# A convolution block in split fp32: the residual stored first and added to by the last transfers, and seven half-size products in one more down stage

## The chip, the cores and the metric

The kernel runs on one core of a Trainium2 chip. The metric is device time in microseconds of one execution; lower is better. Three runs of the kernel before gave a median of 1074.68 (1073.78 to 1074.71). TensorE (PE) multiplies, VectorE (DVE), ScalarE (ACT) and GpSimd (POOL) do elementwise work, and SyncE (SP) issues nearly all transfers, in one queue.

## The reference

One layer with a convolution mixer and an MLP, 256 tokens of width 2048, all in fp32:

```
cond = silu(c)
sh1, sc1, g1, sh2, sc2, g2 = split(cond @ mod_w + mod_b, 6)
h = rms_norm(x, norm1_g) * (1 + sc1) + sh1
x = x + (1 + g1) * conv_mixer(h)                       # two products, a 31-tap convolution, a layer norm
h = rms_norm(x, norm2_g) * (1 + sc2) + sh2
u = square(relu(h @ mlp_w1))                           # 2048 -> 8192
x = x + (1 + g2) * (u @ mlp_w2)                        # 8192 -> 2048
```

Only the MLP's last three quarters and the last line are touched here. The x on the right of the last line is the residual of this document; 1 + g2 is the gate, called `cb` when it is spread over 128 partitions.

## The kernel before

Every fp32 product is made of three products of split operands: an operand is hi (rounded to a type that TensorE reads at full speed) plus lo (the rest), and hi·hi, hi·lo and lo·hi are summed in PSUM (L306 to L308). Weights come from memory as tiles `raw` of 128x2048 (1 MB, seven buffers). ACT makes hi of each half tile (L232), DVE lo (L236, 128x1024), into six buffers of each kind.

The MLP goes through the 8192 inner columns in four quarters q = 0 to 3. Each quarter has an up stage (h times a quarter of mlp_w1) and a down stage (u times a quarter of mlp_w2, added into `y` in SBUF). A job is one step in these stages, with its own weights. A down job, ("down", q, i), has two weight tiles and 48 matmuls of 128x512: i // 2 is one of four blocks of 512 output columns, i % 2 the half of the inner dimension. For q < 3 the order is 0, 2, 1, 3, 4 to 7. In the up stages of q = 1, 2, 3 a part is computed with seven products of half-size blocks in place of eight (Strassen's scheme in Winograd's form, jobs "seven", named S1 to S7; U2, U3, U6, U7 are whole jobs among them). In the down stage of q = 3 four weight tiles, named x, w, z and y, are treated in the same way: seven jobs "eight" (called E here), with 12 matmuls each, stand between whole and half jobs by a list (LAST_JOBS). Their weights are sums of tiles, made by DVE in place in `raw` (a chain, L352), and some have sums of blocks of `u2` on the other side (`make_last_sums`).

The result of an up stage has tokens in partitions and must be turned. DVE transposes blocks of 32x32 (L456), SP writes the block to memory (`flat`, L457) and reads it back as eight transfers of 64 KB in pieces of 128 bytes (`two<-flat`, L474). ACT then does relu and square (L483, L484), and hi (L247), DVE lo (L250), which gives `u2`, the input of the down stage. There are four such blocks per quarter, two `u2` tiles each; in the down stage jobs 0 and 2 need blocks 0 and 1, job 1 the rest.

The residual is written to a scratch in memory, `turned`, during q = 0, in an order with features in partitions. In the down stage of q = 2 it is read back, 32 transfers of 64 KB in pieces of 128 bytes (L496), and DVE does y = y * cb and y = y + residual (`scale_y`, L1105 and L1106), 16 operations of 128x512. The down stage of q = 3 finishes each block: product times cb (L410), plus y (L411), store from SP (L412); where a block has one of the seven products, one more operation goes ahead (L409). The gates become a row `gates` in memory after down job 5 of q = 1, and are loaded as `cb` over all partitions (L1427) after job 7.

The order of instructions on each engine is fixed when the program is built. It is the order of the code's calls, with constraints (`issue_after`) and tasks put off to a later job (`at_job`). All the transfers named here are issued by SP, in the order in which they stand in its program, and an issue that must wait holds what stands behind it.

## Time and profile before

The profiled execution took 1076.49 us; its span from the first to the last instruction is 1074.5, at a mean granted TensorE clock of 0.997. The stages of the MLP that matter, from the trace (us):

| stage | from | to | length | TensorE busy | DVE busy | DMA share |
|---|---|---|---|---|---|---|
| up, q=1 | 561.7 | 643.5 | 81.8 | 81.80 | 71.97 | 0.73 |
| down, q=1 | 643.6 | 732.5 | 88.9 | 87.75 | 70.36 | 0.95 |
| up, q=2 | 732.6 | 814.5 | 81.9 | 81.81 | 74.13 | 0.84 |
| down, q=2 | 814.6 | 901.5 | 86.9 | 86.90 | 57.03 | 0.86 |
| up, q=3 | 901.6 | 984.4 | 82.8 | 82.17 | 75.98 | 0.77 |
| down, q=3, and the end | 984.5 | 1074.5 | 90.0 | 84.87 | 73.82 | 0.48 |

How to read the profile: an engine's row gives the start and length of an instruction, its line, the operation, and what it writes and reads (`lo<-raw,hi`). Behind a group stand the total and the mean in ns. A releaser in brackets, `[3.67 <-DMA two<-flat]`, is idle time ahead of the instruction and what ended it. A transfer has two times: SP's issue, and its landing. DMA share is the mean busy share of the 16 DMA engines.

### The profile page before, as it was taken

How to read it: one execution, taken by the hardware profiler on the slowest of the kernel's cores; microseconds unless marked ns; L12 is line 12 of the kernel's file. 1: busy time of each engine (PE TensorE's matmuls, PEld its weight loads, DVE VectorE, ACT ScalarE, POOL GpSimd, SP SyncE). 2: the span in 40 equal slices, each digit the busy share in tenths (PEclk: the TensorE clock that was granted, in tenths of full speed). 3: DMA queues.
4: the chain of work that ended last, by engine and by line, in shares of the span. 5: the costliest groups of instructions: out<-in, count | busy, mean ns of one | idle time of the engine just before them, and what ended most of it. 6: DMA issues, size and time to landing. Idle time of an engine off the chain costs nothing.

```text
span 1074.5 us, 15563 instructions
## 1 busy us (share of the span) xinstructions
PE 1054.7 (98%) x5868; PEld 871.6 (81%) x5868; DVE 870.6 (81%) x1135; ACT 591.3 (55%) x817; POOL 218.2 (20%) x147
## 2 busy tenths in 40 slices
PE   6999999999999999999999999999999999999998
PEld 3888886778799998888888888788888888787886
DVE  5777789988767889868788895899896678899995
ACT  4111298875875686444546574535575534556751
POOL 0000079989599262000000000000000000000000
PEclk8999999999999999999999999999999999999999
DMA  9999997996999977899895889996889983979731
GB/s 381 420 420 420 415 419 307 363 386 239 412 403 399 371 270 275 262 336 304 279 345 196 297 263 295 345 414 195 343 240 346 236 292 120 303 258 344 213 135 59
DMA packets 154333, 331.00 MB, mean 308 GB/s; under 512 B 88465, under 2 KB 114321, under 8 KB 119313
## 3 DMA queue, kind: packets, MB, share of 16 engines
q1 hardware_dynamic: 154112, 329.88, 84.9%
q8 instruction: 46, 0.75, 0.3%
q14 instruction: 29, 0.24, 0.1%
q10 hardware_dynamic: 146, 0.13, 0.0%
HBM read 313.71 MB, written 16.26 MB: 307 GB/s over the span
## 4 chain that ended last, share of the span: by engine, by line
PE 81%; DMA 9%; DVE 6%; ACT 1%; issue 1%; SPq 0%; ACTq 0%; DVEq 0%
PE mm L307 14%; PE mm L306 14%; PE mm L308 14%; DMA raw<-mod_c 7%; PE mm L264 6%; PE mm L265 3%; PE acc L261 3%; PE acc L260 3%; PE acc L262 3%; PE mm L1029 2%; PE row L516 2%; DVE lo L236 2%; PE acc L427 2%; PE acc L428 2%; PE acc L426 1%; DVE raw L608 1%
## 5 line engine op out<-in xcount | busy, mean ns | idle before, releaser
L232 ACT ACTIVATE hi<-raw 128x1024 fp32r<-128x1024 f32 x362 | 372.8, 1056 | 247.0 <-PE mm L308 159.9
L236 DVE TENSOR_TENSOR lo<-raw,hi 128x1024 fp32r<-128x1024 f32 x301 | 357.3, 1218 | 76.5 <-ACT hi L232 76.3
L306 PE MATMUL mm<-hi,u 128*128 128x512 f32 x448 | 174.2, 390 | 1.7 <-ACT hi L232 1.1
L307 PE MATMUL mm<-lo,u 128*128 128x512 f32 x448 | 174.0, 389 | 0.0
L308 PE MATMUL mm<-hi,u 128*128 128x512 f32 x448 | 173.8, 389 | 0.0
L236 POOL TENSOR_TENSOR lo<-raw,hi 128x1024 fp32r<-128x1024 f32 x61 | 157.0, 2599 | 30.7 <-ACT hi L232 30.7
L608 DVE SCALAR_TENSOR_TENSOR raw<-raw,cond 128x2048 f32<-128x2048 f32 x50 | 117.4, 2356 | 31.7 <-DMA raw<-mod_c 31.7
L308 PE MATMUL mm<-hi,hl 128*128 128x512 f32 x288 | 112.1, 389 | 0.0
L307 PE MATMUL mm<-lo,hl 128*128 128x512 f32 x288 | 112.0, 389 | 0.0
L306 PE MATMUL mm<-hi,hl 128*128 128x512 f32 x288 | 112.0, 389 | 0.0
L306 PEld LDWEIGHTS mm<-hi,u 128*128 128x128 f32 x448 | 84.1, 188 | 20.4 <-ACT hi L232 1.8
L308 PEld LDWEIGHTS mm<-hi,u 128*128 128x128 f32 x448 | 84.1, 188 | 17.9 <-DVE u L250 0.4
L307 PEld LDWEIGHTS mm<-lo,u 128*128 128x128 f32 x448 | 84.1, 188 | 17.4
L908 DVE SCALAR_TENSOR_TENSOR acc<-u,v,acc 128x256 f32<-128x256 f32 x230 | 91.6, 485 | 0.0
L264 PE MATMUL mm<-hl,hi 128*128 128x512 f32 x224 | 80.0, 401 | 0.0
L812 PE MATMUL mm<-two,first 128*128 128x256 f32 x240 | 56.7, 391 | 9.0 <-ACT two L870 9.0
L260 PE MATMUL acc<-hl,hi 128*128 128x256 f32 x224 | 63.4, 283 | 0.0
L261 PE MATMUL acc<-hl,hi 128*128 128x256 f32 x224 | 63.4, 283 | 0.0
L262 PE MATMUL acc<-hl,lo 128*128 128x256 f32 x224 | 63.4, 283 | 0.0
L306 PEld LDWEIGHTS mm<-hi,hl 128*128 128x128 f32 x288 | 54.1, 188 | 11.3
L307 PEld LDWEIGHTS mm<-lo,hl 128*128 128x128 f32 x288 | 54.1, 188 | 11.2
L308 PEld LDWEIGHTS mm<-hi,hl 128*128 128x128 f32 x288 | 54.1, 188 | 11.2
(315 smaller groups left out, 1762.0 us busy)
## 6 DMA issues: line engine op xcount, KB each, us to landing
raw<-w SPq DMA_DIRECT2D x128, 1024.0 KB, 7.3
raw<-mod_c SPq DMA_DIRECT2D x64, 1024.0 KB, 11.5
raw<-mod_r SPq DMA_DIRECT2D x28, 1024.0 KB, 9.1
raw<-w_in SPq DMA_DIRECT2D x16, 1024.0 KB, 10.8
raw<-w_out SPq DMA_DIRECT2D x16, 1024.0 KB, 8.2
first<-w_first SPq DMA_DIRECT2D x15, 1024.0 KB, 19.8
u<-kept SPq DMA_DIRECT2D x24, 512.0 KB, 7.8
flat<-two SPq DMA_DIRECT2D x30, 256.0 KB, 6.0
```

Of the source, the lines that this page charges most:

```text
L232: state["w_hi"] = nc.scalar.activation(hi, w[:, ks, :], AF.Copy).ins
L236: end = by.tensor_tensor(lo, w[:, ks, :], hi.bitcast(F32), op=ALU.subtract)
L260: nc.tensor.matmul(out_p, w, m[:, 0:T], start=begin, stop=False)
L261: nc.tensor.matmul(out_p, w, m[:, T : 2 * T], start=False, stop=False)
L262: state["mm_end"] = nc.tensor.matmul(out_p, lo[:, k % HALF, :], m[:, 0:T], start=False, stop=end)
L264: nc.tensor.matmul(p[:, c, :], hi[:, k % HALF, :], m, start=(k == 0), stop=(k == KT - 1))
L306: nc.tensor.matmul(p, p_hi, hi, start=begin, stop=False, skip_group_check=shared)
L307: nc.tensor.matmul(p, p_hi, lo, start=False, stop=False, skip_group_check=shared)
L308: nc.tensor.matmul(p, p_lo, hi, start=False, stop=end, skip_group_check=shared)
L608: end = nc.vector.scalar_tensor_tensor(w, w, 1.0, cb, op0=ALU.mult, op1=ALU.mult, accum_out=acc)
L812: step = nc.tensor.matmul(held[n][:, c, :], w[:, 2 * n + c, :], h, start=k == 0 and c == 0, stop=k == KT - 1, skip_group_check=True)
L908: end = nc.vector.scalar_tensor_tensor(out, s, w, acc, op0=ALU.mult, op1=ALU.add)
```

## The change

It has three parts, in the same program.

1. The down stage of q = 2 uses the seven products as well, on the same four tiles and with the same list of jobs: 372 matmuls in place of 384. The sums of `u2` for it are kept in space that is free at that point: `cond` (the place of `cb`), `v`, `cz`, `shz`, `rowsb`, `q5` and `two`. The load of `cb` therefore moves from the end of the down stage of q = 1 to the end of that of q = 2. A function `drain` adds the products into y.
2. The residual is no longer read back. Eight transfers (`residual_out`) copy it from the scratch to the output, memory to memory, 256 KB each in 2048 pieces of 128 bytes. They are issued by SP at the jobs in COPY_OUT, all in the up stage of q = 1. The output lies in memory in its final order (tokens by columns).
3. For the first three blocks of columns, the last stage computes (product + y) * cb on DVE, and a transfer from POOL's queue adds it to the output in memory (`accum_op`). For the last block, y * cb is made ahead, at job 3 of the last down stage, two transfers from POOL add the residual from the output to it, and the end is as it was: product times cb, plus y, store.

```diff
--- before
+++ after
...
 PLUS = {5: "w", 7: "z", 6: "z", 4: "y"}
 LAST_JOBS = (4, (1,), 6, (5,), (7,), (3,), 5, (6,), (2,), 1, (4,), 3, 7)
+EIGHT = (2, 3)
 TILE_OF = {"x": (2, 0), "w": (0, 0), "z": (0, 1), "y": (2, 1)}
 MORE = {(0, 0): (1, ALU.add), (0, 1): (5, ALU.add), (1, 1): (7, ALU.subtract)}
+ADDED = 3
+COPY_OUT = [("up", 1, m) for m in (2, 3, 6, 7)] + [("seven", 1, m) for m in (3, 6, 2, 4)]
 OPERAND = {1: "x", 5: "x", 6: "x", 4: "x", 7: "w", 3: "z", 2: "y"}
...
 
     def regions(job):
-        if job[:2] != ("down", QUARTERS - 1):
+        if job[0] == "up" or job[1] not in EIGHT or job[1] < QUARTERS - 1 and job[2] >= 4:
             p = ps.tile([P, 2, 2 * T], F32, name="mm", bufs=2)
...
             at = HALF * (job[2] % 2) + k
             m = acts_of[at // 2][:, at % 2, :]
-            begin, end = at == 0 or job == ("down", QUARTERS - 1, 1) and t == 1 and at == HALF, at == KT - 1
-            shared = job[:2] == ("down", QUARTERS - 1)
+            shared = job[0] == "down" and job[1] in EIGHT
+            begin, end = at == 0 or shared and job[2] == 1 and t == 1 and at == HALF, at == KT - 1
             p_hi, p_lo = [m[:, n : n + P] for n in (t * P, T + t * P)]
...
         if m == 1:
             run_tasks()
-        split_w(("eight", m), nc.vector, chain[name])
+        split_w(("eight", q, m), nc.vector, chain[name])
         if m in (7, 4):
...
 
-    def mm_eight(p, m):
+    def mm_eight(p, q, m):
         for k in range(4):
-            hi, lo = [w[:, 4 * (k % 2) : 4 * (k % 2) + 4, :].rearrange("p k n -> p (k n)") for w in parts["eight", m][k // 2]]
+            hi, lo = [w[:, 4 * (k % 2) : 4 * (k % 2) + 4, :].rearrange("p k n -> p (k n)") for w in parts["eight", q, m][k // 2]]
             if m in (1, 2, 4):
                 at, t = k + (0 if m == 1 else 4), P if m == 4 else 0
                 p_hi, p_lo = [u2[at // 2][:, at % 2, n : n + P] for n in (t, T + t)]
             else:
-                t = P if m in (7, 3) else 0
-                p_hi, p_lo = [last_sums[k // 2, m in (6, 3)][:, k % 2, n : n + P] for n in (t, T + t)]
+                p_hi, p_lo = [s[:, k % 2, :] for s in half_sums[k // 2, m]]
             begin, end = k == 0 and m not in (2, 3), k == 3
...
         return parts_of
 
-    def make_last_sums(k2):
-        work = [acts.tile([P, 2, 2 * T], F32, name="hl", bufs=HALF) for _ in range(2)]
-        _, _, c, d = four_sums(u2[k2], u2[2 + k2], [w[:, :, n : n + T] for w in work for n in (0, T)])
-        for j, src in enumerate((c, d)):
-            last_sums[k2, bool(j)] = acts.tile([P, 2, 2 * T], F32R, name="hl", bufs=HALF)
-            split_act(last_sums[k2, bool(j)], src)
+    def pairs_in(s, n):
+        return [s[:, 2 * T * j : 2 * T * j + 2 * T].rearrange("p (a t) -> p a t", a=2) for j in range(n)]
+
+    def homes(q, k2):
+        if q == QUARTERS - 1:
+            both = [acts.tile([P, 2, 2 * T], F32R, name="hl", bufs=HALF) for _ in range(2)]
+            return [(s[:, :, 0:T], s[:, :, T : 2 * T]) for s in both]
+        if k2 == 0:
+            s = pairs_in(const.tile([P, KT, P], F32R, name="cond").rearrange("p k n -> p (k n)"), 4)
+        else:
+            s = pairs_in(const.tile([P, NVEC], F32R, name="v"), 2)
+            s += pairs_in(const.tile([P, KT, 35], F32R, name="cz").rearrange("p k n -> p (k n)"), 1)
+            s += pairs_in(x_pool.tile([P, KT, 32], F32R, name="shz").rearrange("p k n -> p (k n)"), 1)
+        return [s[0::2], s[1::2]]
+
+    def make_half_sums(q, k2):
+        if q == QUARTERS - 1:
+            work = acts.tile([P, 2, 2 * T], F32, name="hl", bufs=HALF)
+            a, b = work[:, :, 0:T], work[:, :, T : 2 * T]
+        elif k2 == 1:
+            a, b = two(), two()
+        else:
+            work = tmp.tile([P, 512], F32, name="rowsb", bufs=1), mp.tile([P, 512], F32, name="q5", bufs=1)
+            a, b = [s.rearrange("p (a t) -> p a t", a=2) for s in work]
+        for dst, src in ((a, u2[k2]), (b, u2[2 + k2])):
+            nc.vector.tensor_tensor(dst, src[:, :, 0:T].bitcast(F32), src[:, :, T : 2 * T].bitcast(F32), op=ALU.add)
+        (a0, a1), (b0, b1) = [(s[:, :, 0:P], s[:, :, P : 2 * P]) for s in (a, b)]
+        for dst, y0, y1 in ((b1, a1, b1), (a1, a1, a0), (a0, a0, b1), (b0, b0, a0)):
+            nc.vector.tensor_tensor(dst, y0, y1, op=ALU.subtract)
+        for src, (hi, lo), ms in zip((b, a), homes(q, k2), ((3, 5), (6, 7))):
+            nc.scalar.activation(hi, src, AF.Copy)
+            state["sums_end"] = nc.vector.tensor_tensor(lo, src, hi.bitcast(F32), op=ALU.subtract).ins
+            for h, m in enumerate(ms):
+                half_sums[k2, m] = [s[:, :, h * P : h * P + P] for s in (hi, lo)]
 
...
         nc.vector.tensor_tensor(kept_of[5], kept_of[5], w, op=ALU.add)
+
+    def drain(n, t, cs, p):
+        s = y[:, t, 512 * n + cs.start : 512 * n + cs.stop]
+        with tc.issue_after(state["y_end"].ins) if "y_end" in state else ExitStack():
+            state["y_end"] = nc.vector.tensor_tensor(s, p, s, op=ALU.add)
+            if (n, t) in MORE:
+                m, op = MORE[n, t]
+                state["y_end"] = nc.vector.tensor_tensor(s, s, kept_of[m], op=op)
 
...
                 m, op = MORE[n, t]
                 nc.vector.tensor_tensor(g, p, kept_of[m], op=op)
-            nc.vector.tensor_tensor(g, g if (n, t) in MORE else p, cb[:, at], op=ALU.mult)
+                p = g
+            if n < ADDED:
+                nc.vector.tensor_tensor(g, p, s, op=ALU.add)
+                p = g
+            state["y_end"] = nc.vector.tensor_tensor(g, p, cb[:, at], op=ALU.mult)
+        if n < ADDED:
+            nc.gpsimd.dma_start(rows_out[:, t, at], g, accum_op=ALU.add)
+            return
         state["y_end"] = nc.vector.tensor_tensor(s, s, g, op=ALU.add)
-        nc.sync.dma_start(out[:, t, at], s)
+        nc.sync.dma_start(rows_out[:, t, at], s)
+
+    def residual_out(b):
+        with tc.issue_after(state["load"].ins):
+            nc.sync.dma_start(
+                out[32 * b : 32 * b + 32, :].rearrange("p (f t) -> p f t", t=32),
+                turned[:, :, 32 * b : 32 * b + 32].rearrange("k (a p) t -> p (k a) t", p=32),
+            )
 
...
             k2 = 2 * n + h
             u2[k2] = mp.tile([P, 2, 2 * T], F32R, name="u2", bufs=HALF)
-            split_act(u2[k2], s)
-
-    def fetch(n):
-        pieces = []
-        for t in range(2):
-            b = two().rearrange("p a t -> p (a t)")
-            for g in range(4):
-                nc.sync.dma_start(
-                    b[32 * g : 32 * g + 32, :].rearrange("p (a t) -> p a t", t=32),
-                    turned[4 * n : 4 * n + 4, :, 32 * (4 * t + g) : 32 * (4 * t + g) + 32].rearrange("k (a p) t -> p (k a) t", p=32),
-                )
-            pieces.append(b)
-        return pieces
+            with tc.issue_after(state["sums_end"]) if (q, n) == (2, 2) else ExitStack():
+                split_act(u2[k2], s)
 
...
         else:
             jobs += [("up", q, i) for i in range(HALF)]
-        if q < QUARTERS - 1:
+        if q in EIGHT:
+            jobs += [("eight", q) + m if isinstance(m, tuple) else ("down", q, m) for m in LAST_JOBS]
+        else:
             jobs += [("down", q, i) for i in (0, 2, 1, 3, 4, 5, 6, 7)]
-        else:
-            jobs += [("eight",) + m if isinstance(m, tuple) else ("down", q, m) for m in LAST_JOBS]
     def by_tokens(job):
...
             turn_out(flat, t, p)
         if n == 3:
-            read_block(at + (4 if q == QUARTERS - 1 else 1), q, n, flat)
+            read_block(at + {2: 5, 3: 4}.get(q, 1), q, n, flat)
         else:
...
             nc.vector.tensor_tensor(kept_of[7], bank[4], kept_of[7], op=ALU.subtract)
             turn_out(kept_of["flats"][0], 1, kept_of[7])
-            read_block(at + (3 if q == QUARTERS - 1 else 2), q, 2, kept_of["flats"][0])
-
-    def scale_y(s, at, piece):
-        nc.vector.tensor_tensor(s, s, cb[:, at], op=ALU.mult)
-        nc.vector.tensor_tensor(s, s, piece, op=ALU.add)
-
+            read_block(at + (3 if q in EIGHT else 2), q, 2, kept_of["flats"][0])
+
+    rows_out = out.rearrange("(t p) d -> p t d", t=2)
     tasks = {}
     state["job"] = KT + HALF - 2
-    chain, sums_of, kept_of, last_sums = {}, {}, {}, {}
+    chain, sums_of, kept_of, half_sums = {}, {}, {}, {}
 
...
                 copy_wide(COPY_AT[n], False)
         kind, i = job[0], job[-1]
+        if job in COPY_OUT:
+            residual_out(COPY_OUT.index(job))
         if kind == "seven":
...
             elif i % 2 and job[1] in SEVEN:
                 at_job(n + 1, block_out, n + 1, job[1], i // 2, sums.pop((kind, i // 2)))
-                for k2 in range(2) if job == ("up", QUARTERS - 1, 7) else ():
-                    at_job(n + 1, make_last_sums, k2)
+                for k2 in range(2) if i == 7 and job[1] in EIGHT else ():
+                    at_job(n + 1, make_half_sums, job[1], k2)
             elif i % 2:
...
                 with tc.issue_after(state["load"].ins):
                     nc.sync.dma_start(gates[0].rearrange("(k p) -> p k", p=P), modc[:, G2 * KT : G2 * KT + KT])
-            if job == ("down", 1, 7):
+            if job == ("down", 2, 7):
+                cb = const.tile([P, KT, P], F32, name="cond").rearrange("p k n -> p (k n)")
                 with tc.issue_after(state["load"].ins):
                     nc.sync.dma_start(cb, gates.to_broadcast([P, D]))
-            if job[1] == 2 and i % 2 == 0:
-                with tc.issue_after(state["load"].ins):
-                    pieces[i // 2] = fetch(i // 2)
+            if job == ("down", QUARTERS - 1, 3):
+                for t in range(2):
+                    last_y = y[:, t, 512 * ADDED :]
+                    with tc.issue_after(state["w_lo"]):
+                        nc.vector.tensor_tensor(last_y, last_y, cb[:, 512 * ADDED :], op=ALU.mult)
+                    nc.gpsimd.dma_start(last_y, rows_out[:, t, 512 * ADDED :], accum_op=ALU.add)
             if i % 2 == 0:
...
                 if job[1] == 0:
                     nc.scalar.activation(s, p, AF.Copy)
-                elif job[1] < QUARTERS - 1:
+                elif job[1] not in EIGHT:
                     state["drain"] = nc.vector.tensor_tensor(s, p, s, op=ALU.add).ins
-                    if job[1] == 2 and i < HALF - 1:
-                        scale_y(s, at, pieces[i // 2][t])
-                    elif job[1] == 2:
-                        at_job(n + 4, scale_y, s, at, pieces[i // 2][t])
-                elif i in (1, 5):
-                    at_job(n + 1, finish, i // 2, t, cs, p)
                 else:
-                    finish(i // 2, t, cs, p)
+                    end = finish if job[1] == QUARTERS - 1 else drain
+                    if i in (1, 5):
+                        at_job(n + 1, end, i // 2, t, cs, p)
+                    else:
+                        end(i // 2, t, cs, p)
 
```

The order of SP's program around the end of the up stage of q = 1 and the first jobs of the down stage. Names: `raw<-w` is a weight tile, `raw<-mod_c` a weight tile of the gates, `flat<-two` a block written to be turned, `two<-flat` its reading, `out<-turned` a piece of the residual. Before:

```order
L208 DMA raw<-w 128x2048 x3
L457 DMA flat<-two 128x4x128
L208 DMA raw<-w 128x2048 x2
L457 DMA flat<-two 128x4x128
L208 DMA raw<-mod_c 128x2048 x2
L474 DMA two<-flat 32x16x32 x8
```

Now:

```order
L461 DMA out<-turned 2048x1x32
L211 DMA raw<-w 128x2048
L461 DMA out<-turned 2048x1x32
L211 DMA raw<-w 128x2048 x2
L461 DMA out<-turned 2048x1x32
L509 DMA flat<-two 128x4x128
L211 DMA raw<-w 128x2048 x2
L461 DMA out<-turned 2048x1x32
L509 DMA flat<-two 128x4x128
L211 DMA raw<-mod_c 128x2048 x2
L461 DMA out<-turned 2048x1x32
L526 DMA two<-flat 32x16x32 x8
```

Five of the eight pieces now stand among these rows, all ahead of the eight readings; the other three stand earlier in the stage.

DVE's program near the middle of the down stage of q = 2. `x` is y's place, `lo<-raw,hi` a split of half a weight tile, `raw<-raw` a sum of weight tiles. Before:

```order
L236 TENSOR_TENSOR lo<-raw,hi 128x1024 x10
L1105 TENSOR_TENSOR x_2504<-x_2504,cond 128x512 x2
L236 TENSOR_TENSOR lo<-raw,hi 128x1024 x2
L1106 TENSOR_TENSOR x_2504<-x_2504,two 128x512 x2
L236 TENSOR_TENSOR lo<-raw,hi 128x1024 x3
```

Now:

```order
L239 TENSOR_TENSOR lo<-raw,hi 128x1024
L355 TENSOR_TENSOR raw<-raw 128x2048
L429 TENSOR_TENSOR pad<-acc,rowsb 128x512
L430 TENSOR_TENSOR q_7425<-q_7425,pad 128x512
L239 TENSOR_TENSOR lo<-raw,hi 128x1024 x5
L435 TENSOR_TENSOR x_2504<-row,x_2504 128x512
L438 TENSOR_TENSOR x_2504<-x_2504,rowsb 128x512
L435 TENSOR_TENSOR x_2504<-acc,x_2504 128x512
L239 TENSOR_TENSOR lo<-raw,hi 128x1024
L438 TENSOR_TENSOR x_2504<-x_2504,q_7425 128x512
```

The scaling by the gates and the addition of the residual are gone from here; in their place stand sums of weight tiles, what follows the eighth products, and additions into y with a second term.

22 lines of the change are left out of this document (10 added, 12 removed).

## The prediction

> **What bounds the kernel now.** I read first the busy times on the page, then the MLP by its six stages (up and down of quarters 1, 2 and 3, a view by stretches), then TensorE's waits in the MLP, and last the queue around the places where the change adds work.
>
> ```profile
> PE 1054.7 (98%) x5868; PEld 871.6 (81%) x5868; DVE 870.6 (81%) x1135; ACT 591.3 (55%) x817; POOL 218.2 (20%) x147
> ```
>
> TensorE (PE) is busy for 98% of the span of 1074.5. The stages, with the columns stretch, length, busy time (instructions) of PE, weight loads, DVE, ACT and POOL, granted clock, DMA share and GB/s:
>
> ```profile
> 561.70:643.50 81.80, 81.80 (x361) 67.43 (x360) 71.97 (x65) 52.70 (x60) 0.00 (x0) 1.00 0.73 248
> 643.60:732.50 88.90, 87.75 (x385) 71.75 (x384) 70.36 (x75) 40.15 (x44) 0.00 (x0) 1.00 0.95 338
> 732.60:814.50 81.90, 81.81 (x361) 67.42 (x360) 74.13 (x69) 52.07 (x58) 0.00 (x0) 1.00 0.84 281
> 814.60:901.50 86.90, 86.90 (x385) 71.97 (x384) 57.03 (x58) 40.29 (x44) 0.00 (x0) 1.00 0.86 266
> 901.60:984.40 82.80, 82.17 (x361) 67.39 (x361) 75.98 (x72) 51.84 (x58) 0.00 (x0) 1.00 0.77 254
> 984.50:1074.50 90.00, 84.87 (x373) 69.53 (x371) 73.82 (x83) 43.36 (x51) 0.00 (x0) 1.00 0.48 157
> ```
>
> Two readings. Row four, the down stage of q=2, has no idle TensorE at all: 384 matmuls in 86.90, that is 0.2263 us each, so each matmul left out there is worth 0.2263 us if nothing else comes late. Row two, the down stage of q=1, is the one in which the DMA engines have nothing to spare: share 0.95. What stalls TensorE in the MLP is small; columns: total, times, longest.
>
> ```profile
> PE mm L306 <- ACT hi L232: 1.1, 1, 1.1
> PE mm L306 <- DVE two L456: 0.6, 1, 0.6
> PE row L426 <- DMA u<-kept: 0.5, 1, 0.5
> ```
>
> So the number of matmuls sets the time as long as splits, transposes and transfers keep a small lead. The question is which lead the change uses up.
>
> **Matmuls removed: -2.7.** The eight half-tile products that four of q=2's down tiles need (96 matmuls) become seven eight-jobs of 12 each (84). 12 x 0.2263 = 2.7 us.
>
> **Vector work added in q=2's down stage: nothing but one stall of 0.6.** Prices by form, from the groups of DVE from 600 us on (busy, mean ns):
>
> ```profile
> L236 DVE TENSOR_TENSOR lo<-raw,hi 128x1024 fp32r<-128x1024 f32 x209 | 247.9, 1218 | 65.0 <-ACT hi L232 65.0
> L352 DVE TENSOR_TENSOR raw<-raw 128x2048 f32<-128x2048 f32 x4 | 9.1, 2286 | 0.0
> L1106 DVE TENSOR_TENSOR x<-x,two 128x512 f32<-128x512 f32 x8 | 5.3, 684 | 0.0
> L386 DVE TENSOR_TENSOR hl<-hl 128x256 f32<-128x256 f32 x8 | 3.2, 416 | 0.0
> L250 DVE TENSOR_TENSOR hl<-hl 128x512 fp32r<-128x512 f32 x4 | 2.8, 689 | 0.0
> L380 DVE TENSOR_TENSOR hl<-u 128x512 f32<-128x512 f32 x4 | 2.6, 687 | 0.0
> ```
>
> Added: three more weight tiles to split (seven operands out of four tiles), 6 halves x 1.22 = 7.3; four chain sums x 2.29 = 9.1; the half sums of u2 for two k2, each 2 x 0.69 + 4 x 0.42 + 2 x 0.69 = 4.4, so 8.8; three operations after job E6 and three extra drains, 6 x 0.68 = 4.1. Removed: the 16 operations of scale_y (L1106's eight and as many multiplications of the same form), 10.9. Net +18.4: 57.0 becomes 75.4 in a stage of 84.2, 90%. The row of up in q=2 shows 74.1 in 81.9 without a stall, so this can be carried; q=3's down, which runs the same job list, shows one stall for a late transpose, the 0.6 us of the waits above. I take that 0.6 here too. Below nothing it cannot go (the stage has no stall to lose); above, I let it be 2.0, because here the half sums' places (cond, v, cz, shz) are in other buffers and four lo halves of a job stand behind them. ACT gets six more hi, 6 x 1.06, at 40 of 87 us busy: nothing.
>
> **The fetches that go: -0.5.** Before, 32 transfers of 512 pieces bring the residual in, the last eight of them among the first weights of up q=3; columns start, us:
>
> ```profile
> 914.50 2.30 SPq L496 DMA_DIRECT2D two<-turned  x4
> 916.90 2.00 SPq L208 DMA_DIRECT2D raw<-w  x1
> 918.94 2.71 SPq L496 DMA_DIRECT2D two<-turned  x4
> ...
> 923.82 0.85 SPq L444 DMA_DIRECT2D u<-kept  x2
> ```
>
> The sums that they push back (u<-kept) are what TensorE waited for, 0.5 us, in that stage. I take it as gone. The gates' broadcast of 1 MB now stands a quarter later, in the start of up q=3; in the same place of up q=2 it hid (81.81 of 81.90 busy). The one wait added there is for `cond`, which now holds half sums until the eight-jobs have run; the last of them stands two whole down jobs before that load, so the weights queued behind it on SP aren't held. Nothing for it.
>
> **The residual stored ahead: +7.7.** This is the large term. Eight transfers from DRAM to DRAM (out<-turned, 2048 pieces of 128 bytes each) go into SP's queue in up q=1; by the order, five of them stand between the last weights and transposes of that stage, which in the trace are these, and all ahead of the eight two<-flat at 652.41:
>
> ```profile
> 632.10 1.58 SPq L208 DMA_DIRECT2D raw<-w  x3
> 633.78 0.46 SPq L457 DMA_DIRECT2D flat<-two  x1
> 635.26 2.60 SPq L208 DMA_DIRECT2D raw<-w  x2
> 641.89 0.38 SPq L457 DMA_DIRECT2D flat<-two  x1
> 644.13 3.20 SPq L208 DMA_DIRECT2D raw<-mod_c  x2
> 652.41 7.16 SPq L474 DMA_DIRECT2D two<-flat  x8
> ```
>
> In this very stretch the engines have no room (first row: a stretch with room, where the third of the eight falls; the first two stand still earlier; I put all three at nothing, and they cost their length each, some 6 us in all, if the weights then had no lead):
>
> ```profile
> 605.00:610.00 5.00, 5.00 (x23) 4.14 (x23) 3.50 (x5) 3.40 (x4) 0.00 (x0) 1.00 0.46 129
> 630.00:635.00 5.00, 5.00 (x24) 4.14 (x23) 5.00 (x6) 4.51 (x6) 0.00 (x0) 1.00 0.94 238
> 640.00:645.00 5.00, 5.00 (x24) 4.14 (x23) 4.45 (x6) 4.00 (x5) 0.00 (x0) 1.00 1.03 397
> ```
>
> The flat written at 641.89 landed 10.5 us after its issue, at 652.4, and SP issued the reads of it at 652.41, at once:
>
> ```profile
> L457 SPq DMA_DIRECT2D flat<-two x1: 377/377/377, 641.9 to 641.9; - x1
> ...
> DMA to landing us min/median/max: 6.0/8.3/10.5
> ```
>
> So whatever is put ahead of it in this queue moves it by its full length, if the queue is served in order. What is late next: the block's read, its relu and square, its hi and lo, and then TensorE, in whose down job 1 this block is the first input.
>
> ```profile
> 662.83 0.68 DVE L250 TENSOR_TENSOR u<-two,u 128x512 fp32r<-128x512 f32 x1
> 643.60 0.39 PE L306 MATMUL mm<-hi,u 128*128 128x512 f32 x1
> ```
>
> The lo is ready at 663.51; jobs 0 and 2 cover until 643.60 + 96 x 0.2263 = 665.3. The lead is 1.8 us.
>
> One residual transfer, p: the nearest rows are the pieces of 128 bytes of two<-flat. From 618.5 to 621.8 nothing else ran:
>
> ```profile
> q1 hardware_dynamic: 2276, 0.28, 56.6%
> ```
>
> 2276 packets in 56.6% of 16 engines x 3.3 us is 13.1 ns each; 128 pieces per engine make 1.68 us, the lower bound. Issuing such pieces took 2.30 us for four transfers of 512 (the row at 914.50), and 7.16 for eight in the row at 652.41, 3.58 per 2048. I take 1.9: the queue is backed up there, so engines decide and not the issue, with a little for pieces that are written to DRAM as well. 5 x 1.9 - 1.8 = +7.7. After that the weights behind are as late as TensorE is, so they add nothing more.
>
> Against this change speaks the Trainium skill, "DMA: Bandwidth & Descriptors", Specifications: a transfer needs at least 512 bytes for line rate, and below that the DMA does a read-modify-write. By it a 128-byte piece written to DRAM would cost more than one read from it; the trace has such small writes only in the gates (below), which were slow, so it agrees as far as it goes. By that rule the sum would be rival C's.
>
> **The end: nothing.** Three of four blocks of columns now leave through accumulating transfers from POOL, six of 256 KB. The last column ends as before (multiplication, the addition at 1070.72, its store); the last accumulate comes from the column before, and two more bring the residual into the last column of y, behind the last lo:
>
> ```profile
> 1054.77 1.23 DVE L236 TENSOR_TENSOR lo<-raw,hi 128x1024 fp32r<-128x1024 f32 x1 [0.46 <-ACT hi L232]
> ...
> 1061.22 0.69 DVE L411 TENSOR_TENSOR x<-x,two 128x512 f32<-128x512 f32 x1
> ...
> 1065.28 0.69 DVE L411 TENSOR_TENSOR x<-x,two 128x512 f32<-128x512 f32 x1
> ...
> 1070.72 0.69 DVE L411 TENSOR_TENSOR x<-x,two 128x512 f32<-128x512 f32 x1
> ...
> out<-x SPq DMA_DIRECT2D x8, 256.0 KB, 2.0
> ...
> gates<-modc SPq DMA_DIRECT2D x1, 8.0 KB, 17.5
> ```
>
> The last accumulate has from 1061.9 to the span's end at 1074.5 as cover, 12.6 us, for what takes 2.0 as a plain store. Those into y stand behind two more multiplications (0.7 each) after the lo of 1054.77, so from 1057.4 to the addition at 1065.28: 7.9 us. If they took as long as the slowest small transfer, 17.5, the end would come 9.6 late, and if they gain nothing it is 0; they are whole rows of 2 KB as the store's are, so I take 0. "DMA: Bandwidth & Descriptors" of the Trainium skill, Anatomy of one DMA — SWDGE (gpsimd) path, would give an estimate of 2.6 us for 256 KB, which no run here shows for an accumulate.
>
> **Sum.** -2.7 + 0.6 - 0.5 + 7.7 = +5.1. The profiled execution took 1076.49 with its span of 1074.5; 2.0 lie around the span. It would become a span of 1079.6 and 1081.6. The profiled one stands 1.8 above the median of the three runs, 1074.68, so the time forecast is 1079.8. Its own range: four transfers of 1.68 give 6.7 - 1.8 = +4.9 in place of 7.7, 1077.0; five of 3.58 give 17.9 - 1.8 = +16.1, 1088.2.
>
> **Rivals.**
> B, the delay is hidden, and the change is faster. It decides where the five together push the flat back by less than 1.8 us, so below 0.4 each: if the backlog at 641.89 is only weights fetched ahead, and transfers share the engines rather than queue. For it: share 0.46 at 605, so part may land earlier; TensorE was never idle in this stage. Against: the landing after 10.5 us. Then -2.7 + 0.6 - 0.5 = -2.6: 1072.1. Chance 0.27.
> D, DVE bounds the new down stage. For it: 90% busy over the whole, and the half sums and chain sums crowd in its first two thirds. Against: up q=2. With the delay hidden and stalls of 3.2 in place of 0.6 it comes to 1074.7. Chance 0.12.
> C, pieces of 128 bytes are slow to write. For it: the gates' 2048 pieces of 4 bytes took 17.5 us to land while the queue carried little else. From 727 to 738:
>
> ```profile
> q1 hardware_dynamic: 2221, 0.84, 65.1%
> ```
>
> 65.1% of 16 x 11 us over 2221 packets is 52 ns each, 6.6 us for 128 per engine. 5 x 6.6 - 1.8 = 31, so 1074.7 - 2.6 + 31 = 1103. Against: 4 bytes are far from 128, and two<-flat moves 128 at 13.1 ns. Chance 0.07.
> E, the end waits for accumulates, the delay being hidden: with half of the 9.6, -2.6 + 4.8 = +2.2, 1076.9. For it: POOL issues no transfer in this part of the trace, and none accumulates. Against: the cover. Chance 0.08.
> The forecast itself (A): 0.46.
>
> **Range and chances.** 0.2% (2.1 us) is about what a measurement of this kernel can tell from no change. Faster needs B with its stall small: 0.21. Same: the rest of B (0.06), most of D (0.10), half of E (0.04) and a little of the forecast (0.02): 0.22. Slower: the rest of the forecast, C and what is left of D and E: 0.57. The range takes in B below (1072.1, and 1.1 for the stall of 0.6 and the 0.5 not being there) and the forecast's upper bound of 1088 with some of C: 1071 to 1091.
>
> **What would show it.** After the change the last flat of up q=1 lands about 20 us after its issue and TensorE stalls 6 to 9 us near 665, ended by ACT or DVE for that u2: A. A stall there under 1 us: B. DMA share near 1 with few GB/s from 631 on and a stall over 20: C. The down stage of q=2 should be 84.2 to 86 long with 372 matmuls; longer by DVE's waits: D. Between the last finish and the end of the span 3 us as before; more: E. If the five transfers land spread out and the flat still lands within 12 us, my reading of the queue is wrong.

## The result, and the profile after

The changed kernel takes 1088.37 us (median of 4, 1086.27 to 1088.90) beside 1074.26 (4 runs of the kernel before, 1073.78 to 1074.71): a ratio of 1.0128, 95% interval 1.011 to 1.0145, so 14.1 us slower where 5.1 were forecast. Its profiled execution is the shortest of the four, 1086.27 with a span of 1084.5; that of the kernel before was, at 1076.49, longer than its timed runs. The two traces therefore explain 10.0 us (spans 1074.5 and 1084.5); the other 4 lie between executions of the same kernel and are taken up at the end of the experiments.

The page of the changed kernel, first section, and its six stages from q=1 on (same columns as before):

```profile
PE 1055.8 (97%) x5856; PEld 870.6 (80%) x5856; DVE 890.8 (82%) x1153; ACT 598.5 (55%) x829; POOL 223.9 (21%) x155
```

```profile
561.30:643.18 81.88, 81.88 (x361) 67.51 (x360) 72.72 (x65) 51.83 (x59) 0.00 (x0) 1.00 0.83 252
643.18:740.86 97.68, 89.54 (x385) 73.28 (x384) 70.50 (x76) 41.12 (x46) 0.00 (x0) 0.97 0.96 335
740.86:822.84 81.98, 81.90 (x362) 67.51 (x360) 74.38 (x69) 52.05 (x58) 0.00 (x0) 1.00 0.81 270
822.84:910.20 87.36, 85.96 (x373) 69.55 (x372) 76.33 (x79) 48.75 (x56) 0.00 (x0) 1.00 0.72 246
910.20:992.22 82.02, 81.94 (x362) 67.42 (x360) 74.09 (x69) 51.93 (x58) 0.00 (x0) 1.00 0.76 265
992.22:1084.50 92.28, 84.89 (x373) 69.55 (x371) 74.55 (x84) 42.85 (x51) 7.22 (x8) 0.97 0.57 158
```

Set beside the rows of before, three stages differ. Down q=1 grew from 88.9 to 97.7. Down q=2 should have shrunk from 86.9 to 84.2 and is 87.4: 12 matmuls fewer, and all of their 2.7 us lost again, with some 0.4 more. The last stage grew from 90.0 to 92.3. Up q=3 is 0.8 or 0.9 shorter. The longest waits of TensorE are

```profile
PE mm L309 <- ACT u L250: 7.3, 1, 7.3
PE mm L310 <- DVE lo L239: 1.1, 1, 1.1
PE mm L309 <- DVE x L1482: 0.8, 1, 0.8
```

The first and the third stand in down q=1, the second in down q=2.

**Down q=1.** SP's queue around the last flats of up q=1 (start, length of the issue):

```profile
642.78 0.55 SPq L461 DMA_DIRECT2D out<-turned  x1
643.42 6.24 SPq L509 DMA_DIRECT2D flat<-two  x1
649.75 1.28 SPq L211 DMA_DIRECT2D raw<-w  x2
651.08 0.55 SPq L461 DMA_DIRECT2D out<-turned  x1
651.73 5.96 SPq L509 DMA_DIRECT2D flat<-two  x1
657.78 0.95 SPq L211 DMA_DIRECT2D raw<-mod_c  x2
658.79 0.55 SPq L461 DMA_DIRECT2D out<-turned  x1
660.04 9.39 SPq L526 DMA_DIRECT2D two<-flat  x8
```

The issue of a copy takes 0.55, but the transfer behind it isn't taken for 6 us: the two flats hold SP for 6.24 and 5.96 where they took 0.46 and 0.38. I read this as a queue that has no room left; no view shows its filling. The second flat lands 8.3 us after the start of its issue (651.73 + 8.3 = 660.0), before it landed at 652.4: 7.6 us later, behind four copies (the fifth stands behind this flat and ahead of its reading). So one copy costs 1.9 us. TensorE stands still for 7.3 us, and then something follows that the waits don't show. Stretches of the stall, of what comes behind it, and of the eight-jobs in down q=2:

```profile
664.70:672.40 7.70, 0.41 (x2) 0.00 (x0) 0.01 (x1) 2.45 (x5) 0.00 (x0) 0.82 0.89 174
672.40:676.70 4.30, 4.29 (x11) 3.34 (x12) 3.79 (x5) 3.96 (x5) 0.00 (x0) 0.53 1.00 361
850.00:856.00 6.00, 4.60 (x16) 2.50 (x15) 6.00 (x8) 6.00 (x10) 0.00 (x0) 1.00 0.86 332
```

In the second row the granted clock is 0.53: from the first matmul behind the stall, at 672.41, to the one at 676.69 ten steps take 4.3 us where 2.3 were due, 2.0 us on top of the stall. The Trainium skill, "TensorE: Matmul & The Clock Gate", Part 1: The HAM clock gate, states such a rule: after an idle window of about 3.4 us the clock is halved until TensorE has been busy for about as long. By that rule a stall of 7.3 us carries a slow stretch with it; the trace agrees, 7.3 us idle and 4.3 at about half. The rule does not cover what the first experiment below shows, where two stalls of 1.2 us halve the clock as well.

**Down q=2.** The third row: from 850 to 856 DVE is busy for all of 6.00 us, ACT as well, and TensorE for 4.60. The row alone doesn't tell which of the two TensorE is behind.

**The end.** POOL's transfers, and the last addition on DVE:

```profile
1066.28 0.88 POOL L1473 DMA_DIRECT2D x<-out  x1 [3.32 <-issue]
1070.61 0.90 POOL L1473 DMA_DIRECT2D x<-out  x1 [3.45 <-issue]
1074.95 0.88 POOL L454 DMA_DIRECT2D out<-two  x1 [3.44 <-issue]
1079.16 0.89 POOL L454 DMA_DIRECT2D out<-two  x1 [3.34 <-DVE x L456]
```

```profile
1077.95 0.69 DVE L456 TENSOR_TENSOR x<-x,two 128x512 f32<-128x512 f32 x1
```

They start 4.3 us apart though their data were ready long before (the last one's at 1069.1, by the order of DVE's operations). From the end of the last addition to the end of the span it is 5.9 us (1078.6 to 1084.5); before it was 3.1 (1071.4 to 1074.5).

So the 10.0 us are: -2.7 for the matmuls, +7.5 the stall (its step less one matmul), +2.0 the slow clock, -0.8 for small stalls of down q=1 that went or moved, +3.1 lost in down q=2 (what is left of that stage; its matmuls' steps show 2.7 of it between 850 and 856), -0.9 in up q=3, -0.5 for the stall of the last stage that is shorter, +2.8 at the end, and -0.4 ahead of these stages: 10.1. (Stages are counted from first matmul to first matmul; before, these stood at 561.7, 643.6, 732.6, 814.6, 901.6 and 984.5.)

### The profile page after: what moved, and what is told of

Its sections match the earlier page's. It is cut to its first block, busy times and chain, and to the rows that moved or that the text cites. A ratio compares the mean times of both kernels' runs of the same rounds, so it can differ in the third digit from the quotient of the medians.

```text
span 1084.5 us, 15550 instructions
## 1 busy us (share of the span) xinstructions
PE 1055.8 (97%) x5856; PEld 870.6 (80%) x5856; DVE 890.8 (82%) x1153; ACT 598.5 (55%) x829; POOL 223.9 (21%) x155
## 4 chain that ended last, share of the span: by engine, by line
PE 73%; DMA 11%; DVE 9%; issue 2%; ACT 2%; SPq 2%; POOLq 0%; POOL 0%; ACTq 0%; DVEq 0%
PE mm L310 11%; PE mm L311 11%; PE mm L309 11%; DMA raw<-mod_c 7%; PE mm L267 6%; PE mm L268 3%; DVE lo L239 3%; PE acc L264 2%; PE acc L263 2%; PE acc L265 2%; PE mm L1070 2%; DMA flat<-two 2%; DVE raw L649 2%; PE row L557 2%; SPq L526 2%
## 5 line engine op out<-in xcount | busy, mean ns | idle before, releaser
L235 ACT ACTIVATE hi<-raw 128x1024 fp32r<-128x1024 f32 x368 | 377.2, 1054 | 231.8 <-PE mm L311 124.7
L239 DVE TENSOR_TENSOR lo<-raw,hi 128x1024 fp32r<-128x1024 f32 x307 | 363.4, 1216 | 49.7 <-ACT hi L235 49.0
L309 PE MATMUL mm<-hi,u 128*128 128x512 f32 x384 | 150.5, 393 | 8.4 <-ACT u L250 7.3
L310 PE MATMUL mm<-lo,u 128*128 128x512 f32 x384 | 150.2, 391 | 1.1 <-DVE lo L239 1.1
L311 PE MATMUL mm<-hi,u 128*128 128x512 f32 x384 | 149.5, 391 | 0.0
L454 POOL DMA_DIRECT2D out<-two x6 | 5.4, 906 | 653.8 <-DVE two L452 642.2
L309 PEld LDWEIGHTS mm<-hi,u 128*128 128x128 f32 x384 | 72.6, 189 | 25.2 <-ACT u L250 7.7
L310 PEld LDWEIGHTS mm<-lo,u 128*128 128x128 f32 x384 | 72.6, 189 | 16.7 <-DVE lo L239 1.6
L311 PEld LDWEIGHTS mm<-hi,u 128*128 128x128 f32 x384 | 72.5, 189 | 15.1 <-DVE u L253 0.2
L310 PEld LDWEIGHTS mm<-lo,hl 128*128 128x128 f32 x288 | 54.1, 188 | 11.3
L309 PEld LDWEIGHTS mm<-hi,hl 128*128 128x128 f32 x288 | 54.1, 188 | 11.2
```

The lines of the kernel that those rows point to most:

```text
L235: state["w_hi"] = nc.scalar.activation(hi, w[:, ks, :], AF.Copy).ins
L239: end = by.tensor_tensor(lo, w[:, ks, :], hi.bitcast(F32), op=ALU.subtract)
L309: nc.tensor.matmul(p, p_hi, hi, start=begin, stop=False, skip_group_check=shared)
L310: nc.tensor.matmul(p, p_hi, lo, start=False, stop=False, skip_group_check=shared)
L311: nc.tensor.matmul(p, p_lo, hi, start=False, stop=end, skip_group_check=shared)
```

## The experiments

The theory after this: each copy ahead of the last flat costs 1.9 us of queue, and the stall brings the slow clock; POOL's transfers run one after another; DVE is too busy in down q=2. The first rivals: the copies cost wherever they stand, and the loss in down q=2 comes from being late. Each run was timed beside the kernel before, whose median lay between 1074.26 and 1075.71, and the ratios go by that; a difference of about 1 us between the medians of two runs says little. The 2.2 and 9.7 in some expectations are the slow clock and the loss of down q=1 as they were first read; by the matmuls' steps they are 2.0 and 9.5.

**Copies moved to three up stages.**

```diff
-COPY_OUT = [("up", 1, m) for m in (2, 3, 6, 7)] + [("seven", 1, m) for m in (3, 6, 2, 4)]
+COPY_OUT = [(kind, q, m) for q in (1, 2, 3) for kind, m in (("up", 2), ("seven", 3), ("up", 3))][:8]
```

> All eight residual copies stand behind the second, third and early jobs of the up stages of quarters 1, 2 and 3 (three, three and two), none near the last flats of up q=1. Theory (each copy ahead of the last flat delays it by 1.95 us in SP's queue; five of them less a lead of 1.8 made the 7.5 us stall, and the slow clock behind it 2.2 more): the stall at 664.7 and the stretch at clock 0.53 go, 9.7 us less, about 1078.7. Rival 1 (the DMA engines' total work counts, not the place in the queue): the loss moves into up q=2 and q=3 with their shares of 0.84 and 0.77, time 1086 to 1088. Rival 2 (128-byte writes slow the memory): the same 1086 to 1088, with stalls wherever the copies stand.

Measured: 1083.76 (1080.78 to 1084.84), ratio 1.0079 (1.0066 to 1.0092). The stall of 7.3 and its slow clock are gone, but only 4.6 us of 9.5 came back. In its trace up q=1 is 0.7 longer than in the changed kernel's, up q=2 1.3 and down q=2 2.8. In down q=2 its waits are now

```profile
PE mm L310 <- DVE lo L239: 1.2, 1, 1.2
PE acc L375 <- ACT v L421: 1.2, 1, 1.2
PE mm L309 <- ACT u L250: 1.1, 1, 1.1
```

The last is the first input of that stage, late behind the copies in up q=2. The two others fall within 2 us and halve the clock for 8 matmuls (427 ns from one to the next). Part of rival 1 holds: copies cost in up q=2 too, by delaying u2.

**The transfers into y ahead of all stores.**

```diff
-            if job == ("down", QUARTERS - 1, 3):
+            if job == ("down", QUARTERS - 1, 4):
```

> The two transfers that add the residual into the last block of y are made at the first job of the last down stage in place of its job 3, so that they stand ahead of all six accumulating stores on POOL's queue. Theory (these transfers run one after another, 4.3 us apart, whatever their data; the last one is late because of the two in front of it): the last accumulate lands before the last plain store, 2.8 us less, 1085.6. Rival (an accumulating store is slow in landing by itself, or POOL's end of program takes the time): unchanged, 1088.4.

Measured: 1084.69 (1082.74 to 1086.09), ratio 1.009 (1.0076 to 1.0103); 3.7 below the changed kernel. POOL's last two, in its trace:

```profile
1068.41 0.87 POOL L454 DMA_DIRECT2D out<-two  x1 [4.51 <-DVE two L452]
1072.65 0.88 POOL L454 DMA_DIRECT2D out<-two  x1 [3.37 <-issue]
```

They are still 4.2 apart, but the last one is out before the last addition (1078.9), and the span ends 3.2 us after that, as in the kernel before. The last stage takes 89.8 where the changed kernel's took 92.3. The term for the end is shown.

**Seven products undone in q=2.**

```diff
-EIGHT = (2, 3)
+EIGHT = (3,)
...
-            read_block(at + {2: 5, 3: 4}.get(q, 1), q, n, flat)
+            read_block(at + {3: 4}.get(q, 1), q, n, flat)
```

The constraint that held back the third block's u2 goes with them.

> The seven half-size products are undone in q=2 (the residual part of the change stays). Theory (the products saved 2.7 us of TensorE and lost 2.9 to a DVE that was busy without a gap from 844 to 860): 1088.4 + 2.7 - 2.9 = 1088.2, no stall in the down stage of q=2, 86.9 long. Rival (those stalls come from the stage being late and out of step after the 7.5 us stall, not from DVE's load): a loss of 2.7 shows, 1091, or stalls in the plain stage as well.

Measured: 1087.84 (1086.34 to 1089.56), ratio 1.0121 (1.0108 to 1.0134), so no difference from the changed kernel. But the stage wasn't free of stalls, against the expectation:

```profile
PE mm L309 <- ACT u L250: 1.5, 1, 1.5
```

That is the fourth block's u2, read behind two weight tiles. The products gained nothing here, for this and for the reason expected; this run doesn't separate the two, the one with the copies moved as well, further on, does.

**The kernel before, once more** (no edit).

> The kernel before itself, for a second profile beside the first (whose execution, 1076.5, was 2.2 above the median of its runs): 1074.3 in the median; if its stalls of 1.3 at 689 and 0.9 at 930 are steady they are there again, and if they are what made the first profile longer, they are gone.

Measured: 1074.44 (12 runs, 1073.15 to 1076.92). In its trace, with a span of 1073.0, the waits are

```profile
PE mm L306 <- ACT hi L232: 1.2, 1, 1.2
PE mm L306 <- DVE two L456: 0.6, 1, 0.6
```

The wait for hi, at 689 in the first trace, is there again. The wait for `u<-kept` (0.5) isn't. It belonged to that execution, and the gain booked on it, 0.5, was mostly not to be had.

**Two copies in place of five.**

```diff
+COPY_OUT = [("up", 1, 2), ("up", 1, 3)] + [("seven", 1, m) for m in (3, 2, 4)] + [("eight", 2, m) for m in (6, 2, 4)]
```

> Of the five residual copies ahead of the last flats of up q=1 only two stay there; the three early ones of that stage stay too, and the other three go to the end of the down stage of q=2, where the readings of the residual stood in the kernel before. Theory (1.95 us each, lead 1.8): the stall before the third block's u2 falls from 7.5 to 2 x 1.95 - 1.8 = 2.1, and a stall that short leaves no stretch at half clock behind it (2.2): 1088.4 - 5.4 - 2.2 = 1080.8. Rival (the delay does not go by the number of copies; any copy in front of the flat holds the queue till it has landed, about 8 us): stall of 5 or more, 1086.

Measured: 1082.49 (1082.24 to 1085.05), ratio 1.0079 (1.0062 to 1.0095). The stall ahead of the third block is 1.9 us of waiting, 2.05 by the matmuls' steps, where 2.1 was expected:

```profile
PE mm L309 <- ACT u L250: 2.5, 2, 1.9
```

(the second wait in this row, 0.6, is the next block's). Behind it the clock stays at 1.00:

```profile
667.00:671.00 4.00, 3.98 (x16) 3.02 (x17) 3.22 (x4) 3.86 (x5) 0.00 (x0) 1.00 1.01 395
```

Five copies gave 7.5, two give 2.05: 1.8 us each, and the line crosses zero at 0.9 copies, which is a lead of 1.6 us beside the 1.8 of the prediction. The time is 1.7 above the expected one: down q=2 takes 89.3 in this trace, 1.9 more than in the changed kernel's.

**The same bytes in large pieces.**

```diff
-                out[32 * b : 32 * b + 32, :].rearrange("p (f t) -> p f t", t=32),
-                turned[:, :, 32 * b : 32 * b + 32].rearrange("k (a p) t -> p (k a) t", p=32),
+                out[32 * b : 32 * b + 32, :].rearrange("p (f t) -> (p f) t", t=256),
+                turned[2 * b : 2 * b + 2].rearrange("k p t -> (k p) t"),
```

> The eight copies stay at their places with the same 256 KB each, but move contiguous memory, 16 pieces of 16 KB, in place of 2048 of 128 bytes; so the residual lands in another order and the output is not the reference's. Theory (a copy costs by its pieces): 256 KB at the 400 GB/s that the queue reaches there is 0.66 us, twice that if reading and writing share the engines; 5 x 1.0 - 1.8 = 3.2 for the stall in place of 7.5, and less of the half clock: 1082 to 1084. Rival (a copy from memory to memory costs by its bytes or by a fixed time): stall 7.5, 1088.4.

Measured: 1078.99 (1078.22 to 1079.22), ratio 1.0037 (1.0023 to 1.005), 9.4 below the changed kernel. The wait for u2 isn't among its waits at all:

```profile
PE mm L310 <- DVE lo L239: 1.1, 1, 1.1
PE acc L376 <- DVE lo L239: 0.8, 1, 0.8
PE acc L375 <- ACT v L421: 0.7, 1, 0.7
```

I had expected 3.2. The last two flats of up q=1 hold SP for 0.53 and 0.38 us only, and the reading of the block begins at 651.81, no later than before. So with the same places and bytes the copies cost less than the lead, under 0.4 each. The cost goes with the 2048 small pieces and not with the bytes.

**All copies in down q=2, and the transfers into y ahead.**

```diff
+COPY_OUT = [("eight", 2, m) for m in (3, 6, 2, 4)] + [("down", 2, m) for m in (5, 1, 3, 7)]
```

> All eight copies in the down stage of q=2, behind the five first of its jobs (where the kernel before read the residual), and the transfers into the last block of y at the first job of the last stage. Theory: the 9.7 at 665 to 677 go, and no up stage gets a new stall (as up q=2 did when the copies were put there); the end is 3.7 shorter, as measured alone: 1088.4 - 13.4 = 1075.0, with DVE's stall of 2.9 in the down stage of q=2 left; 1078 if the clock falls there as it did with the copies in the three up stages. Rival (copies cost wherever they stand): 1079 or more, with new stalls in the down stage of q=2 or in up q=3.

Measured: 1077.12 (1076.43 to 1079.76), ratio 1.0025 (1.0014 to 1.0035). 11.3 of the 14.1 are back. What its trace, the longest of its nine executions, lost anew is in up q=3, in SP's queue and in its waits there:

```profile
915.49 5.68 SPq L461 DMA_DIRECT2D out<-turned  x2
921.22 1.36 SPq L1467 DMA_DIRECT2D cond<-gates  x1
922.67 0.85 SPq L211 DMA_DIRECT2D raw<-w  x2
```

```profile
PE mm L309 <- ACT hi L235: 1.0, 1, 1.0
PE mm L310 <- DVE lo L239: 0.8, 1, 0.8
```

Two copies and cb's load stand ahead of the weights; two stalls close together, and again the half clock behind them.

**Half of the half sums on POOL.**

```diff
+        by = nc.gpsimd if q == 2 and k2 == 1 else nc.vector
...
-            nc.vector.tensor_tensor(dst, y0, y1, op=ALU.subtract)
+            by.tensor_tensor(dst, y0, y1, op=ALU.subtract)
```

> As the kernel with the copies in the down stage of q=2 and the early transfers into y, and the second half of the half sums of q=2 (two additions, four subtractions, two lo) computed by POOL, which does nothing there, in place of DVE. Theory (the stalls at the eight-jobs M5 and D6 of q=2 are DVE's, which is busy without a gap from 844 to 860, with 4.4 us of these sums among them): the stall falls from 2.9 to under 0.8, about 1072.5. Rival (POOL's slower operations, 2.6 us where DVE takes 1.2, or a port that both share, make the sums or DVE later): the stall stays or grows, 1075 to 1078.

Measured: 1080.18 (1079.09 to 1080.59), ratio 1.0047 (1.0034 to 1.006), 3.1 worse than without. POOL started late and was slow, and DVE was slow beside it:

```profile
833.64 4.15 POOL L417 TENSOR_TENSOR two<-u 128x512 f32<-128x512 f32 x2 [421.37 <-DMA flat<-two]
837.86 6.07 POOL L420 TENSOR_TENSOR two<-two 128x256 f32<-128x256 f32 x4
843.90 1.26 POOL L423 TENSOR_TENSOR shz<-two,v 128x512 fp32r<-128x512 f32 x1
```

```profile
834.96 3.38 DVE L253 TENSOR_TENSOR u<-two,u 128x512 fp32r<-128x512 f32 x2
838.26 5.09 DVE L239 TENSOR_TENSOR lo<-raw,hi 128x1024 fp32r<-128x1024 f32 x3
```

DVE's two 128x512 took 1.69 each (0.69 elsewhere), its splits 1.70 (1.22). That is the rival. The Trainium skill, "Trainium Architecture — The Big Picture", What this means for kernel authors, says that DVE and GpSimd share a port and exclude one another there; the trace agrees in that both are slower together: POOL's two 128x512 took 2.07 us each, and one of that size at 843.90, with DVE idle, took 1.26.

**Three copies in up q=1, five in down q=2.**

```diff
+COPY_OUT = [("up", 1, 2), ("up", 1, 3), ("seven", 1, 3)] + [("eight", 2, m) for m in (3, 6, 2)] + [("down", 2, m) for m in (5, 1)]
```

> The three copies of up q=1 that cost nothing stay there, the other five go to the middle of the down stage of q=2 (none next to the loading of cb), and the early transfers into the last block of y. Theory: what the kernel with all eight in the down stage still lost in up q=3 (two stalls of 1.1 and 1.0 and 1.7 of half clock, since two copies and cb's 1 MB stood together ahead of that stage's weights) goes, 3.9 of its 1077.1: 1073.2, beside 1074.9 for the kernel before. Rival (that loss comes from cb's load alone, which the kernel before had a quarter earlier): 1077.

Measured: 1076.57 (11 runs, 1075.34 to 1079.14) beside 1075.70, ratio 1.0011 (1.0002 to 1.002). The stalls of up q=3 are gone, but its trace, the longest of its executions, has waits that the changed kernel's did not have, one at the start of down q=1 (645.6) and one in up q=1 (630.8):

```profile
PE mm L309 <- ACT u L250: 1.1, 1, 1.1
PE acc L479 <- DVE lo L239: 0.7, 1, 0.7
```

By the steps of the matmuls, six of the twelve traces with copies in up q=1 lose 0.7 to 1.9 us at the start of down q=1, and none of the four without. So the three copies that I had put down as free are so only in some executions. The larger loss is in down q=2, 89.4 long.

**The same without the seven products**, with copies in ("down", 2, 1), 3, 4, 5 and ("up", 3, 2).

> The same care for the copies (three in up q=1, four in the down stage, one in up q=3) and the early transfers into y, with the seven products of q=2 undone. Theory (they save 2.7 and lose 2.9 to DVE): the same time as with them, 1073.4, plus up to 1.6 for the third-block stall that the kernel without the products showed at 856: 1073 to 1075. Rival (the products' loss was due to the lateness in q=1): without them 2.7 slower, 1076 or more.

Measured: 1076.45 (12 runs, 1075.71 to 1080.40), ratio 1.0012 (1.0003 to 1.0022): with and without the products the time is the same, and the residual part by itself, placed with care, gains nothing over the kernel before. In the stage itself the traces differ: down q=2 takes 87.0 here, without a stall, and 89.4 with the products above. So the products cost more there than they save, and the loss of 3.1 in the changed kernel's trace was a small one: in the seven other traces with these products and this order of jobs, all sums made by DVE, the stage takes 88.3 to 90.1. As the late stall is gone from five of the seven, being late isn't the cause. What the run without the products loses elsewhere, some of it in its longer down q=1 (90.6 for 88.5), was not followed up.

**One set of half sums left out.**

```diff
+        if q < QUARTERS - 1 and k2 == 1:
+            half_sums.update({(1, m): half_sums[0, m] for m in (3, 5, 6, 7)})
+            return
```

> As the first of these, but q=2's second set of half sums is left out and the first one used in its place (eight operations of DVE, 4.4 us, and two of ACT less; the result is not the reference's). Theory (the stalls before and in the eight-jobs of q=2 are DVE's load): they fall from 2.9 to under 0.8, about 1071. Rival (they come from late weight tiles or from TensorE's waits for ACT): they stay, 1073.

Measured: 1072.87 (7 runs, 1071.94 to 1074.89) beside 1075.70, ratio 0.9974 (0.9963 to 0.9986), and no wait at all in down q=2, which takes 84.6. The middle of that stage in the kernel with three copies in up q=1 and both sets of sums, and here:

```profile
812.00:860.00 48.00, 45.15 (x191) 35.29 (x191) 42.18 (x48) 29.92 (x40) 0.00 (x0) 1.00 0.85 284
812.00:860.00 48.00, 48.00 (x212) 39.53 (x211) 42.63 (x44) 30.94 (x39) 0.00 (x0) 1.00 0.84 273
```

Eight operations of DVE, 4.4 us, and two of ACT decide over the 2.7 us of the matmuls. Which of the two engines it is stays open: of the three long waits in the first of these traces two end with DVE's splits and one with ACT, both engines lost work by this edit, and in the changed kernel both were busy without a gap from 850 to 856.

**D5 ahead of E5** (the eight-job called M5 in the expectation), with the second set of half sums behind, or between, the splits of the third and fourth block. Both blocks are also read one or two jobs earlier, the constraint on u2 is gone, and one of the five copies stands at another job.

```diff
+MID_JOBS = (4, (1,), 6, 5, (5,), (7,), (3,), (6,), (2,), 1, (4,), 3, 7)
...
-                    at_job(n + 1, make_half_sums, job[1], k2)
+                    at_job(n + (1 if job[1] == QUARTERS - 1 or k2 == 0 else 5), make_half_sums, job[1], k2)
```

> As the kernel with three copies in up q=1, five in the down stage and the early transfers into y; in the down stage of q=2 whole job D5 now stands ahead of eight-job M5, and the second set of half sums is made behind the splits of the third and fourth block. So the half sums are wanted 48 matmuls (10.9 us) later, and DVE's work is the same. Theory (in the first 25 us of that stage DVE has more to do than time before M5; with the sums out of that stretch the stall goes, as when they were left out): 2.9 less than with the old order, about 1073 to 1073.7, beside 1075 to 1075.7 for the kernel before. Rival (DVE's total in the stage, 75.4 of 84.2, is too much in any order): stalls of 2 to 3 elsewhere in that stage, 1076.

> The same, with the second set of half sums one task earlier, between the splits of the third and the fourth block. Theory: as above, within 1 us, with a small stall for the fourth block's u2, which stands behind three of these operations; 1073 to 1074.5. Rival: 1076.

Measured: 1081.12 (1080.15 to 1083.13), ratio 1.0054 (1.0041 to 1.0067), and 1078.10 (1076.70 to 1080.81), ratio 1.0032 (1.002 to 1.0044). In the down stage, the first and then the second of them:

```profile
PE acc L376 <- ACT hi L236: 3.4, 1, 3.4
PE acc L376 <- ACT v L422: 1.0, 1, 1.0
```

```profile
PE acc L378 <- DVE shz L423: 1.7, 1, 1.7
PE mm L312 <- DVE u L254: 1.4, 1, 1.4
```

The stalls move and stay: the rival. In the two orders tried, with the reads moved too, the place doesn't help; what helped was less work. Both waits of the first order end with ACT, so DVE alone isn't shown to be the cause.

**POOL's transfers without adding.**

```diff
-            nc.gpsimd.dma_start(rows_out[:, t, at], g, accum_op=ALU.add)
+            nc.gpsimd.dma_start(rows_out[:, t, at], g)
...
-                    nc.gpsimd.dma_start(last_y, rows_out[:, t, 512 * ADDED :], accum_op=ALU.add)
+                    nc.gpsimd.dma_start(last_y, rows_out[:, t, 512 * ADDED :])
```

> The changed kernel with its eight transfers on POOL's queue made plain (they store or load without adding, so the residual is lost in the output and the result is not the reference's); data, places and queue are the same. Theory: the 4.24 us from one to the next belong to POOL's queue, whatever the transfer does: the last four stand 4.2 apart again and the end is as late, 1088. Rival: adding is what makes one wait for the other, so plain ones follow each other within 1.0 (POOL's issue is 0.9), the end is 2.8 shorter, 1085.

Measured: 1088.72 (1086.05 to 1088.98), ratio 1.0116 (1.0098 to 1.0133). The time is not clearly different (1.0128 for the changed kernel), but the trace settles the question it was run for:

```profile
1069.38 1.15 POOL L1473 DMA_DIRECT2D x<-out  x2 [1.73 <-DVE x L1472]
1072.64 0.55 POOL L454 DMA_DIRECT2D out<-two  x1 [2.10 <-DVE two L452]
```

Two in a row take 1.15, the span ends 3.2 us after the last addition, and the last stage takes 90.5 for 92.3. It is the adding, not POOL's queue, that sets them 4.3 apart, and my theory on that point was wrong. In place of the 2.7 saved this trace has a longer stall at 675 (8.3), one of 1.2 at the start of down q=1, and 0.7 at 1006. All three stand ahead of POOL's first transfer, at 1045.1, so the edit didn't make them.

**The other 4 us.** Up to the last stage the programs of "the transfers into y ahead" and "without adding" are the changed kernel's, so their traces are two more executions of it. From the start of up q=1 to the start of down q=3 they take 431.4 and 435.2 us, the changed kernel's own trace 430.9. The second is 4.3 longer: 1.4 at the end of up q=1, 1.3 in down q=1 and 1.5 in down q=2. So one program does differ by this much from one execution to the next, and in the stages named above: a wait of nothing to 1.2 us at the start of down q=1, 8 to 14 slow matmuls behind the long stall, 2.7 to 4.3 us lost before and in the eight-jobs. The changed kernel's profiled execution was the shortest on each count or close to it.

**What stays open** is why one execution has these waits and another doesn't, and whether DVE or ACT is what TensorE is behind in down q=2.

## Why the prediction was wrong

The direction and the main mechanism were right, the size was not: +5.1 was forecast, +14.1 measured, +10.0 between the traces. What failed are three terms of the sum that stood at nothing or near it: what follows the stall, the vector work, and the end. The time came out at the upper end of the forecast's own range (1088.2), but not for the reason given there: no copy took 3.58.

- *Residual stored ahead, +7.7*: right. The stall measured 7.5; 1.8 to 1.9 us per copy and a lead of 1.6 to 1.8 held, with five copies and with two. The 1.9 had been chosen between 1.68 and 3.58, so that it came so close is in part luck. Of the signs named for it the stall showed and the landing did not: the flat landed 8.3 us after its issue, not 20, and the copies spread out, from 639.6 to 667.6, which by the prediction's last sentence would make its reading of the queue wrong. The order was as read, for these transfers landed in the order of their issues; but the waiting was on SP, ahead of the flat's issue, which began at 651.73 in place of 641.89. That the cost is in the pieces was shown by the large ones. Rival C (slow writes) fell: a piece copied within DRAM costs 1.9 us / 128 = 15 ns, near the 13.1 of a piece read into SBUF. Rival B fell with the landing at 660.0.
- *What follows a stall of that length*: left out of the sum. The clock fell to 0.53 for 4.3 us, 2.0 us more. The sentence "After that the weights behind are as late as TensorE is, so they add nothing more" was true of the weights and not of TensorE.
- *Vector work, one stall of 0.6*: wrong in size; 3.1 were lost, beyond the 2.0 that I allowed, and more in the other traces. I read 75.4 of 84.2 as bearable because up q=2 carries 74.1 of 81.9. The mean was right (76.3 measured) and told nothing: in the first 30 us the sums crowd ahead of E5, and from 850 to 856 neither DVE nor ACT had idle time. I put ACT at nothing by its mean as well (40 of 87). Rival D, which named the crowding, belonged into the sum.
- *The end, nothing*: wrong; it took 2.8. The step took each transfer by itself against its cover and never put the eight behind each other. An accumulating transfer waits for the one before it, 4.3 us each, and lands 3.9 to 4.0 after its issue; the last four need 17 us from 1066.3. Rival E had the place and the mechanism of one slow transfer, not of a chain.
- *Fetches, -0.5*: up q=3 got 0.9 shorter, but in the second trace of the kernel before that stage is 0.5 shorter than in the first, so more than half of it was chance.
- *Matmuls, -2.7*: right, but for small steps. With one set of sums left out down q=2 takes 84.6, without the products 87.0, and neither has a stall there.

## What to carry to other kernels

Here a transfer put into a queue that was already behind cost its full service time to the first transfer behind it that someone waited for, and its cost went by its pieces: count them, and look for the next round trip behind it. Add to a stall of the size seen here (7 to 8 us) the slow clock that followed it in all four traces, and to a stage with high mean load the load in the stretch just ahead of what it must feed. Transfers that add are to be summed as a chain, and the ones without a deadline of their own go first.
